# Bias tables read backward from one copy, longer modulation products, and gate rows sent through memory

## The chip, the cores and the metric

The kernel runs on one core of one Trainium2 chip. Times are microseconds (us) of device time of one launch. TensorE (PE in the profile) multiplies matrices and PEld is its weight load; VectorE (DVE), ScalarE (ACT) and GpSimd (POOL) compute and copy; SyncE (SP) and, in this kernel, also ACT and POOL issue DMA transfers, which 16 DMA engines carry out.

## The reference

Two layers of a hybrid block and one layer of a second block act on 256 tokens of width 2048, all in float32.

```
for layer in range(2):                      # first block
    proj = x @ w_in[layer]                  # 2048 -> 7680, split into 11 parts
    ya = diff_attention(q, k, v, bias)      # 4 heads; bias by distance from rel_bias
    yb = dilated_attention(q, k, v, bias)   # 8 heads; bias by distance
    yc = conformer_conv(...)                # 31 taps, layer norm, 512 x 512
    x = layer_norm(ALPHA * x + concat(ya, yb, yc) @ w_out[layer])
# second block
mod = silu(c) @ w_mod + b_mod               # six vectors of 2048: shifts, scales, two gates
h = modulate(rms_norm(x), mod[0], mod[1])
# neighbourhood attention (bias rpb[head, row offset, column offset]), Fourier, pooling
# and short-convolution branches, merged through sigmoid gates into y
x = x + mod[2] * (y @ w_o)
x = x + mod[5] * swiglu(modulate(rms_norm(x), mod[3], mod[4]))
```

Three parts matter here. The attention heads of the first block add a bias that depends on query minus key position alone, so a head's table is a row of 384 numbers, laid out shifted by one for each query partition. The neighbourhood attention adds such a bias by column offset. The two gate vectors `mod[2]` and `mod[5]` multiply every token's row, so they are wanted as 2048 numbers on each of 128 partitions.

## The kernel before, in words

All weights stream once through SBUF. A job is a weight piece of 512 KB (256 rows by 512 columns), loaded by SP into `raw` (four buffers), split by ACT into a high part `hi` (line 343) and by DVE into the rest `lo` (line 351). A step of the program multiplies one job by the transposed activations: twelve matmuls of 512 columns (hi by high, lo by high, hi by low, for two halves of the rows and two token tiles) into the PSUM tile `mm`. ACT and DVE work up to four steps ahead of TensorE (`LOOK`). There are 892 jobs and as many steps, in the order in which `run` writes them out; every engine takes its own instructions in that order.

Everything else is a side task, a generator that is advanced by one link per step: attention heads, transposes, convolution, norms. Some of them let a step pass when a meter of DVE's work (`room`) says that DVE is behind; the meter counts about 1.04 ns for each element and 0.065 us for each DVE call, so fewer calls can move such work to an earlier step.

The modulation product `mod` is computed on DVE. `wmod_step` takes a job of [128, 1024] numbers of `w_mod` (tile `wm`, two buffers, loaded by SP) and multiplies and sums it against the vector `c` (spread over all partitions) into the accumulator `wsum`. There are 192 jobs, in six chunks that `WMOD_STEPS` spreads over the steps; chunks 0 and 1 are done for two vectors, so there are 256 products of 1024. `wmod_end` finishes a chunk; for chunks 2 and 5, the gates, it makes the tiles `gb` (2048 numbers on each partition).

`bias_tables`, added at step 20, makes the first block's tables. It computes the 12 rows `r` of 384 numbers, writes them to memory as `scr` and reads the three tables `T` from it. `tables`, at step 220, does the like for the second block: it writes `rpbs`, from which `na_head` reads a piece `rpb` twice for each pair of a head and a query tile. POOL issues all of these, in order with its small norm computations (`rstd`) and the residual transfers (`res`, `xs`). `causal` and `na_head` add the tables to the scores on DVE.

Of the kernel before, what the change touches and what calls it, by code (L numbers as in the profile page):

```python
# [18 lines left out]
D = 2048  # L19
# [13 lines left out]
# the order in which the normed (group, token tile) pieces are transposed, and how many a group's use waits for  # L33
TILES = [(0, 0), (1, 0), (0, 1), (1, 1), (2, 0), (2, 1), (3, 0), (3, 1)]
READY = [3, 4, 6, 8]
# the part of the program (in steps) over which each chunk of the modulation's product is spread
# [18 lines left out]
class Meter:  # L55
    """Passes calls on to an engine and adds up about how long they hold it, in us."""
# [30 lines left out]
class Task:  # L87
    """A generator that emits a side chain of the program, a link per step."""
# [24 lines left out]
class Block:  # L113
    """One block of output columns: all of its contraction, for its token tiles."""
# [14 lines left out]
class Kernel:  # L129
# [47 lines left out]
    def room(self):  # L177
        """Time left on the vector engine until the tensor engine is through this step."""
        return self.t_pe + 2.6 - self.t_dve
# [4 lines left out]
    def need(self, t, items=1 << 30):  # L184
        """Emits what is left of a task (or its first items). A task between steps holds no more than
        its `rows` of the row buffers and its `banks` of the four, and what has begun stays within them."""
        if t.done or t.items >= items:
            return
        if t in self.tasks:
            self.tasks.remove(t)  # L190
        if t not in self.running:
            while self.held()[0] + t.rows > ROWS or self.held()[1] + t.banks > 4:
                self.need([r for r in self.running if not r.busy][0])
            self.running.append(t)
        was, t.forced = t.forced, True
        while not t.done and t.items < items:
            t.step()
        t.forced = was
        if t.done:
            self.running.remove(t)  # L200

    def wait(self, me, deps):
        """Lets steps pass until the tasks are done."""
        while not all(t.done for t in deps):
            if me().forced:
                for t in deps:
                    self.need(t)
                break
            yield
# [14 lines left out]
    def rstd(self, var, n, scale, eps):  # L224
        """(var * scale + eps) ** -0.5 for [128, n]."""
# [6 lines left out]
    def split_t(self, items, ahead=0):  # L232
        """Transposes [128 tokens, 512] pieces and splits them. items: (src, hi, lo, scale, bias),
        src a function that gives the piece; scale and bias: [128, 4] columns or None."""
# [72 lines left out]
    def order(jobs):  # L307
        """Steps of four (job, half of its contraction, token tile) each, and the step after which each job's
        operands are free. At the tail of a block its first token tile goes ahead of the second."""
# [96 lines left out]
    def wmod_init(self):  # L406
        """silu(c) @ w_mod + b_mod on the vector engine, 128 of its elements at a time."""
# [7 lines left out]
        self.wm_junk = self.cp.tile([128, 512], BF16, name="wmjunk")  # L415
# [22 lines left out]
    def wmod_step(self, force=False):  # L438
# [14 lines left out]
        if f == 0 and k == 0:  # L453
            self.need(self.wm_task)
            self.wm_sum = [self.m([128, 16, 4], name="wsum", bufs=3) for _ in range(2 if chunk < 2 else 1)]
        t = self.wm_raw.pop(i)
        for v, acc in enumerate(self.wm_sum):
            for q in range(2):
                x = slice(q * 512, (q + 1) * 512)
                nc.vector.tensor_tensor_reduce(out=self.wm_junk, in0=t[:, x], in1=self.wm_c[v][k][:, x], scale=1.0,  # L460
                                               scalar=0.0, op0=ALU.mult, op1=ALU.add,
                                               accum_out=acc[:, f, 2 * k + q:2 * k + q + 1])
# [5 lines left out]
    def wmod_end(self, chunk, sums):  # L468
# [17 lines left out]
        if chunk in (2, 5):  # L486
            yield
            for g in range(4):
                if g % 2 == 0:
                    row = self.modc[(chunk, g // 2)] = self.s([128, 1024], name="gb")  # L490
                p = self.aux()
                for j in range(4):
                    nc.tensor.matmul(p[:, j * 128:(j + 1) * 128], d[:, g * 4 + j:g * 4 + j + 1].broadcast_to([128, 128]),
                                     self.ident, start=True, stop=True)
                yield
                nc.scalar.activation(row[:, (g % 2) * 512:(g % 2 + 1) * 512], p, AF.Copy)
                yield
# [36 lines left out]
    def bias_tables(self):  # L534
# [14 lines left out]
        # 128 copies of each row, read one short of their pitch: row p comes out shifted by p  # L549
        scr = self.dp.tile([12, 128, 384], F32, name="scr")  # L550
        nc.gpsimd.dma_start(scr, r.unsqueeze(1).broadcast_to([12, 128, 384]))
        self.T = []
        for g in (1, 2, 0):
            t = self.s([128, 4, 256], name="T")
            nc.gpsimd.dma_start(t, bass.AP(scr.tensor, g * 4 * 128 * 384 + 127, [[383, 128], [128 * 384, 4], [1, 256]]))
# [222 lines left out]
    def rms_t(self, r, ss, sc, sh, dst=None, rs=None):  # L778
        """rms norm, scale and shift of token-major r (4 of [128, 2, 512]) into transposed halves."""
# [38 lines left out]
    def qk_t(self, q, k, c, scale):  # L818
        """Transposed q (times scale) and k of one head: [128, 512], q then k."""
# [14 lines left out]
    def causal(self, qk, rows, T, s, m, i):  # L834
        """Negated scores of both query tiles: [128, 384] (tile 1, then tile 0) and their minima."""
# [5 lines left out]
        nc.vector.tensor_tensor_reduce(out=s[:, 0:256], in0=p[:, 0:256], in1=T, scale=1.0, scalar=3e38,  # L841
                                       op0=ALU.add, op1=ALU.min, accum_out=m[:, i:i + 1])
        nc.vector.tensor_tensor_reduce(out=s[:, 256:384], in0=p[:, 256:384], in1=T[:, 128:256], scale=1.0, scalar=3e38,
# [10 lines left out]
    def pv(self, s, v, c):  # L854
        """Probabilities [128, 384] times v: PSUM [128, 256], tile 1 then tile 0."""
# [133 lines left out]
    def second(self):  # L989
# [70 lines left out]
        def tables():  # L1060
            self.rpb = self.dp.tile([56, 64, 127], F32, name="rpbs")
            nc.gpsimd.dma_start(self.rpb, a["rpb"].unsqueeze(1).broadcast_to([56, 64, 127]))
# [170 lines left out]
    def context(self):  # L1233
        """Normed and modulated context, transposed and split."""
# [14 lines left out]
    def na_head(self, j, hd, x, y, need, me):  # L1249
# [7 lines left out]
        def load(t):  # L1257
            raw = self.h([128, 256], name="rpb")
            for i in range(2):
                off = (hd * 7 + 3 - 2 * t - i) * 64 * 127 + 63  # L1260
                nc.gpsimd.dma_start(raw[i * 64:(i + 1) * 64, :].rearrange("p (a c) -> p a c", a=4),
                                    bass.AP(self.rpb.tensor, off, [[126, 64], [64 * 127, 4], [1, 64]]))
# [16 lines left out]
        for t in range(2):  # L1279
# [9 lines left out]
                                    raw.rearrange("p (a c) -> p a c", a=4), op=ALU.subtract)  # L1289
# [26 lines left out]
    def put_split(self, p, dst, c, scale=None):  # L1316
        """[128, 256] in PSUM into the halves of chunk c."""
# [121 lines left out]
def _constants():  # L1439
# [5 lines left out]
    c["onehot"] = oh  # L1445
# [4 lines left out]
    c["dmask"] = mask  # L1450
# [21 lines left out]
def _layout(i):  # L1472
# [22 lines left out]
    def blocks(w):  # L1495
        """[.., K, N] as [.., N / 512, K / 256, 128, 1024]: what one transfer brings, in one piece."""
# [10 lines left out]
        "ln_g": n["ln_g"], "ln_b": n["ln_b"], "rel_bias": n["rel_bias"], "rpb": rpb.reshape(56, 127),  # L1507
# [25 lines left out]
```

## Time and profile before

| what | value |
|---|---|
| time, median of 3 runs | 2675.42 us (2675.05 to 2678.34) |
| span of the profiled execution, first to last instruction | 2668.7 us |
| median above that span | 6.7 us |
| TensorE busy | 2624.8 us, 98% of the span |
| weight loads busy | 2164.3 us, 81% |
| VectorE busy | 1843.7 us, 69% |
| ScalarE busy | 1260.4 us, 47% |
| mean DMA rate | 231 GB/s |

For the profiled execution no time other than its span is given, so the time around the span (launch and end) is taken as the 6.7 us between it and the median. Busy time of an engine is the union of its instructions' times. Matmuls overlap each other in a pipeline, so two matmuls that start 0.23 us apart each show a duration of 0.39 us, and TensorE can show no idle time while its matmuls start more slowly than they could.

### The profile page before, as it was taken

To read this page: it belongs to the slowest core of one execution; us is meant where nothing else is said; L and a number is where in the kernel's file an instruction comes from. 1 tells how busy PE (TensorE), PEld (TensorE's weight loads), DVE (VectorE), ACT (ScalarE), POOL (GpSimd) and SP (SyncE) were. 2 spreads that over 40 slices of the span, in tenths; PEclk is the share of its full clock that TensorE was granted. 3 is DMA by queue.
4 is the path that set the end of the run, shared out by engine and by line. 5 is a ranking of instruction groups with operands and counts; after the bars stand their busy time and mean duration, and the time that the engine had idled before them with its cause. 6 is when DMAs were issued, how large, how long until landed. Compare 5 with 4: busy or idle time off the path is not lost.

```text
span 2668.7 us, 33167 instructions
## 1 busy us (share of the span) xinstructions
PE 2624.8 (98%) x11962; PEld 2164.3 (81%) x11962; DVE 1843.7 (69%) x3028; ACT 1260.4 (47%) x1609; POOL 126.1 (5%) x188
## 2 busy tenths in 40 slices
PE   9999999989999999999999999999999999999999
PEld 7788888768888888887888888888788888888887
DVE  5699787769988799664756686778554554555444
ACT  6354654435566556454454444444444434443442
POOL 0000010000000111020200000000100000000000
PEclk9999999999999999999999999999999999999999
DMA  8876667577765778785767787788655566556654
GB/s 304 213 231 219 212 225 251 194 221 233 233 227 195 280 268 286 255 256 184 230 224 237 255 283 260 262 289 305 222 181 190 190 237 205 189 190 240 225 194 154
DMA packets 171749, 616.79 MB, mean 231 GB/s; under 512 B 19994, under 2 KB 20788, under 8 KB 171584
## 3 DMA queue, kind: packets, MB, share of 16 engines
q1 hardware_dynamic: 158400, 572.59, 64.0%
q0 software_dynamic: 11744, 39.29, 5.3%
q10 hardware_dynamic: 1440, 2.79, 0.3%
q8 instruction: 94, 1.54, 0.2%
q14 instruction: 71, 0.58, 0.1%
HBM read 599.64 MB, written 16.76 MB: 231 GB/s over the span
## 4 chain that ended last, share of the span: by engine, by line
PE 87%; DVE 5%; DMA 4%; issue 2%; ACT 1%; POOL 0%; SPq 0%; ACTq 0%; DVEq 0%; POOLq 0%
PE mm L75 82%; PE aux L75 6%; DMA raw<-in_w_in 3%; DVE lo L351 2%; DVE f L75 1%; DVE wmjunk L75 1%; DVE cacc L75 1%; DMA raw<-in_w_out 1%; ACT hi L343 0%; DVE res L75 0%; DMA row<-in_ln_b 0%; DMA row<-in_ln_g 0%; DVE hcTl L75 0%; POOL rstd L229 0%; DVE bn L75 0%
## 5 line engine op out<-in xcount | busy, mean ns | idle before, releaser
L351 DVE TENSOR_TENSOR lo<-raw,hi 128x1024 fp32r<-128x1024 f32 (+1 forms) x893 | 1077.0, 1220 | 629.9 <-ACT hi L343 627.2
L343 ACT ACTIVATE hi<-raw 128x1024 fp32r<-128x1024 f32 (+1 forms) x893 | 937.5, 1059 | 1067.4 <-PE mm L75 777.7
L75 PE MATMUL mm<-hi,xTh 128*128 128x512 f32 x960 | 388.0, 404 | 18.3 <-ACT hi L343 18.3
L75 PE MATMUL mm<-lo,xTh 128*128 128x512 f32 x960 | 379.0, 395 | 3.5 <-DVE lo L351 3.5
L75 PE MATMUL mm<-hi,xTl 128*128 128x512 f32 x960 | 379.1, 395 | 0.6 <-DVE xTl L75 0.6
L75 DVE CUSTOM_DVE_ANT_0 wmjunk<-wm,c 128x512 bf16<-128x512 f32 x512 | 352.9, 689 | 13.1 <-DMA wm<-in_w_mod 1.9
L75 PE MATMUL mm<-hi,hTh 128*128 128x512 f32 x864 | 343.9, 398 | 0.0
L75 PE MATMUL mm<-hi,hTl 128*128 128x512 f32 x864 | 337.1, 390 | 0.0
L75 PE MATMUL mm<-lo,hTh 128*128 128x512 f32 x864 | 336.6, 390 | 0.0
L75 PE MATMUL mm<-hi,h2Th 128*128 128x512 f32 x704 | 275.9, 392 | 1.1 <-ACT h2Th L284 1.1
L75 PE MATMUL mm<-hi,h2Tl 128*128 128x512 f32 x704 | 274.4, 390 | 1.1 <-DVE h2Tl L75 1.1
L75 PE MATMUL mm<-lo,h2Th 128*128 128x512 f32 x704 | 274.2, 389 | 0.0
L75 PEld LDWEIGHTS mm<-hi,xTh 128*128 128x128 f32 x960 | 183.0, 191 | 57.9 <-ACT hi L343 20.0
L75 PEld LDWEIGHTS mm<-lo,xTh 128*128 128x128 f32 x960 | 183.2, 191 | 42.0 <-DVE lo L351 6.4
L75 PEld LDWEIGHTS mm<-hi,xTl 128*128 128x128 f32 x960 | 182.6, 190 | 40.5 <-DVE xTl L75 1.3
L75 PEld LDWEIGHTS mm<-hi,hTl 128*128 128x128 f32 x864 | 162.2, 188 | 34.5
L75 PEld LDWEIGHTS mm<-lo,hTh 128*128 128x128 f32 x864 | 162.5, 188 | 32.4 <-issue 0.2
L75 PEld LDWEIGHTS mm<-hi,hTh 128*128 128x128 f32 x864 | 162.4, 188 | 32.3 <-issue 0.2
L75 PEld LDWEIGHTS mm<-hi,h2Tl 128*128 128x128 f32 x704 | 132.2, 188 | 29.0 <-DVE h2Tl L75 1.5
L75 PEld LDWEIGHTS mm<-hi,h2Th 128*128 128x128 f32 x704 | 132.2, 188 | 28.3 <-ACT h2Th L284 1.6
L75 PEld LDWEIGHTS mm<-lo,h2Th 128*128 128x128 f32 x704 | 132.3, 188 | 26.9
L75 PE MATMUL mm<-hi,yTh 128*128 128x512 f32 x384 | 151.2, 394 | 0.0
(273 smaller groups left out, 3094.9 us busy)
## 6 DMA issues: line engine op xcount, KB each, us to landing
raw<-in_w_in SPq DMA_DIRECT2D x360, 512.0 KB, 4.4
wm<-in_w_mod SPq DMA_DIRECT2D x192, 512.0 KB, 4.7
raw<-in_w_gate SPq DMA_DIRECT2D x128, 512.0 KB, 4.5
raw<-in_w_fg SPq DMA_DIRECT2D x88, 512.0 KB, 4.3
raw<-in_w_fu SPq DMA_DIRECT2D x88, 512.0 KB, 3.9
raw<-in_w_fd SPq DMA_DIRECT2D x88, 512.0 KB, 4.2
raw<-in_w_out SPq DMA_DIRECT2D x64, 512.0 KB, 4.6
raw<-in_w_o SPq DMA_DIRECT2D x32, 512.0 KB, 5.1
```

The source lines that it names most:

```text
L75: return f(*args, **kw)
L343: nc.scalar.activation(hi[:, k], t[:, k], AF.Copy)
L351: nc.nc.vector.tensor_tensor(lo[:, k], t[:, k], hi[:, k], op=ALU.subtract)
```

## The change

1. The table rows are computed in reverse order (the constants `onehot` and `dmask` are reversed). They are written to memory once (12 rows of 384 numbers) where there were 128 copies of each, and `T` reads a window that starts one number later for each partition. `causal` then reads `T` backward along its columns.
2. `rpb` comes reversed from the host, and `na_head` reads its pieces straight from that input; the copy `rpbs` is gone. The DVE subtraction reads `raw` backward.
3. A modulation product of 1024 is one DVE operation instead of two of 512.
4. For the gates, one matmul turns the [128, 16] vector into 16 rows of 128, ACT copies them to `grow`, a DMA writes them to memory as `g`, and two broadcast DMAs read `gb` from it. Before, 16 matmuls of 128 columns and four ACT copies for each gate made the same numbers on the chip.

```diff
@@ wmod_step
-            self.wm_sum = [self.m([128, 16, 4], name="wsum", bufs=3) for _ in range(2 if chunk < 2 else 1)]
+            self.wm_sum = [self.m([128, 16, 2], name="wsum", bufs=3) for _ in range(2 if chunk < 2 else 1)]
         t = self.wm_raw.pop(i)
         for v, acc in enumerate(self.wm_sum):
-            for q in range(2):
-                x = slice(q * 512, (q + 1) * 512)
-                nc.vector.tensor_tensor_reduce(out=self.wm_junk, in0=t[:, x], in1=self.wm_c[v][k][:, x], scale=1.0,
-                                               scalar=0.0, op0=ALU.mult, op1=ALU.add,
-                                               accum_out=acc[:, f, 2 * k + q:2 * k + q + 1])
+            nc.vector.tensor_tensor_reduce(out=self.wm_junk, in0=t, in1=self.wm_c[v][k], scale=1.0, scalar=0.0,
+                                           op0=ALU.mult, op1=ALU.add, accum_out=acc[:, f, k:k + 1])
@@ wmod_end, chunks 2 and 5
-            for g in range(4):
-                if g % 2 == 0:
-                    row = self.modc[(chunk, g // 2)] = self.s([128, 1024], name="gb")
-                p = self.aux()
-                for j in range(4):
-                    nc.tensor.matmul(p[:, j * 128:(j + 1) * 128], d[:, g * 4 + j:g * 4 + j + 1].broadcast_to([128, 128]),
-                                     self.ident, start=True, stop=True)
-                yield
-                nc.scalar.activation(row[:, (g % 2) * 512:(g % 2 + 1) * 512], p, AF.Copy)
-                yield
+            p = self.aux()
+            nc.tensor.matmul(p[0:16, 0:128], d, self.ident, start=True, stop=True)
+            yield
+            r = self.m([16, 128], name="grow", bufs=2)
+            nc.scalar.activation(r, p[0:16, 0:128], AF.Copy)
+            yield
+            g = self.dp.tile([1, D], F32, name=f"g{chunk}")
+            nc.gpsimd.dma_start(g.rearrange("o (f e) -> (o f) e", e=128), r)
+            yield
+            for i in range(2):
+                row = self.modc[(chunk, i)] = self.s([128, 1024], name="gb")
+                nc.gpsimd.dma_start(row, g[:, i * 1024:(i + 1) * 1024].broadcast_to([128, 1024]))
+            yield
+            yield
@@ bias_tables
-        scr = self.dp.tile([12, 128, 384], F32, name="scr")
-        nc.gpsimd.dma_start(scr, r.unsqueeze(1).broadcast_to([12, 128, 384]))
+        scr = self.dp.tile([12, 384], F32, name="scr")
+        nc.gpsimd.dma_start(scr, r)
...
-            nc.gpsimd.dma_start(t, bass.AP(scr.tensor, g * 4 * 128 * 384 + 127, [[383, 128], [128 * 384, 4], [1, 256]]))
+            nc.gpsimd.dma_start(t, bass.AP(scr.tensor, g * 4 * 384 + 1, [[1, 128], [384, 4], [1, 256]]))
@@ causal (the 128-column operation alike)
-        nc.vector.tensor_tensor_reduce(out=s[:, 0:256], in0=p[:, 0:256], in1=T, scale=1.0, scalar=3e38,
+        nc.vector.tensor_tensor_reduce(out=s[:, 0:256], in0=p[:, 0:256], in1=T[:, ::-1], scale=1.0, scalar=3e38,
@@ second
-            self.rpb = self.dp.tile([56, 64, 127], F32, name="rpbs")
-            nc.gpsimd.dma_start(self.rpb, a["rpb"].unsqueeze(1).broadcast_to([56, 64, 127]))
@@ na_head
-                                    bass.AP(self.rpb.tensor, off, [[126, 64], [64 * 127, 4], [1, 64]]))
+                                    bass.AP(a["rpb"].tensor, off, [[1, 64], [127, 4], [1, 64]]))
...
-                                    raw.rearrange("p (a c) -> p a c", a=4), op=ALU.subtract)
+                                    raw.rearrange("p (a c) -> p a c", a=4)[:, :, ::-1], op=ALU.subtract)
```

On TensorE the order of all other matmuls is as it was. The first place is the first gate burst, in the stage of the `w_gate` weights; `wcol` is the gate vector, `aux` the PSUM tile of side tasks. Before:

```order
L75 MATMUL mm<-hi,hTl 128x512
L75 MATMUL aux<-ident,wcol 128x128 x4
L75 MATMUL mm<-hi,hTh 128x512
L75 MATMUL mm<-lo,hTh 128x512
L75 MATMUL mm<-hi,hTl 128x512
```

and with the change:

```order
L75 MATMUL mm<-hi,hTl 128x512
L75 MATMUL aux<-ident,wcol 16x128
L75 MATMUL mm<-hi,hTh 128x512
L75 MATMUL mm<-lo,hTh 128x512
L75 MATMUL mm<-hi,hTl 128x512
```

There were four such bursts of four matmuls for each gate; one matmul for each gate is left, and nothing else moved.

The second place is POOL at the first block's tables; `mk` is a constant, `rstd` the first norm after them. Before:

```order
L541 DMA mk<-in_dmask 12x384
L551 DMA scr<-r 1536x1x384
L555 DMA T<-scr 128x4x256 x3
L228 ISA
L228 TENSOR_SCALAR rstd<-cmv 128x1
```

and with the change:

```order
L542 DMA mk<-in_dmask 12x384
L553 DMA scr<-r 12x384
L557 DMA T<-scr 128x4x256 x3
L228 ISA
L228 TENSOR_SCALAR rstd<-cmv 128x1
```

The order is the same, and the first transfer writes 12 rows where it wrote 1536. Where the second block's copy `rpbs` stood, POOL has nothing in its place.

The third place is POOL at the end of the second block's `w_o` stage, with the change. `xs_o` and `res` are the residual's transfers, `rstd` belongs to the norm ahead of the last stage, and all rows but the two of line 492 and 496 stood there before in the same order.

```order
L1177 DMA xs_o<-res 128x512 x2
L1158 DMA res<-xs_8043 128x2x512
L492 DMA g_15278<-grow 16x128
L496 DMA gb<-g_15278 128x1024 x2
L1177 DMA xs_o<-res 128x512 x2
L1158 DMA res<-xs_8043 128x2x512
L228 TENSOR_SCALAR rstd<-tot 128x1
```

Three DMAs of the second gate are thus ahead of the last residual transfers and of that norm. Those of the first gate stand in a long stretch in which POOL has nothing else.

## Rows read from the trace of the kernel before

**Rows 1.** The page: span, and TensorE's busy time and weight loads

```profile
span 2668.7 us, 33167 instructions
...
PE 2624.8 (98%) x11962; PEld 2164.3 (81%) x11962; DVE 1843.7 (69%) x3028; ACT 1260.4 (47%) x1609; POOL 126.1 (5%) x188
```

**Rows 2.** The chain that ended last, in order of time: start us, us, what

```profile
84.80 26.66 DMA raw<-in_w_in
...
565.53 25.66 DMA raw<-in_w_in
...
2606.99 57.17 PE mm L75 x252
```

**Rows 3.** POOL in order of time: start us, us, instruction, idle before and releaser

```profile
75.29 1.11 POOL L551 DMA_DIRECT2D scr<-r  x1 [72.23 <-DVE r L75]
111.92 2.29 POOL L555 DMA_DIRECT2D T<-scr  x3 [35.53 <-DMA scr<-r]
...
560.28 1.72 POOL L1062 DMA_DIRECT2D rpbs<-in_rpb  x1
```

**Rows 4.** DMA issues: name, queue, count, KB each, median us to landing

```profile
c<-in_c ACTq DMA_DIRECT2D x4, 512.0 KB, 11.0
...
scr<-r POOLq DMA_DIRECT2D x1, 2304.0 KB, 36.4
...
rpbs<-in_rpb POOLq DMA_DIRECT2D x1, 1778.0 KB, 30.5
T<-scr POOLq DMA_DIRECT2D x3, 512.0 KB, 5.7
```

**Rows 5.** TensorE in order of time, where the two stalls begin

```profile
98.41 0.39 PE L75 MATMUL mm<-hi,xTl 128*128 128x512 f32 x1
...
578.93 0.39 PE L75 MATMUL mm<-hi,xTl 128*128 128x512 f32 x1
588.57 0.80 PE L75 MATMUL mm<-hi,xTh 128*128 128x512 f32 x1 [9.26 <-ACT hi L343]
```

**Rows 6.** Windows: length; busy (count) of PE PEld DVE ACT POOL; clock, DMA share, GB/s

```profile
98.41:128.50 30.09, 24.59 (x88) 18.10 (x86) 17.79 (x31) 11.34 (x12) 2.29 (x3) 0.89 0.85 248
579.15:604.00 24.85, 15.13 (x58) 11.81 (x58) 13.53 (x24) 9.46 (x10) 0.00 (x0) 0.79 0.66 199
2000.00:2100.00 100.00, 100.00 (x451) 82.83 (x450) 48.37 (x44) 44.05 (x47) 0.00 (x0) 1.00 0.58 189
130.00:400.00 270.00, 269.23 (x1282) 221.71 (x1281) 237.22 (x515) 152.51 (x252) 11.26 (x16) 1.00 0.68 222
```

**Rows 7.** TensorE in order of time at the first gate burst

```profile
1710.38 1.05 PE L75 MATMUL aux<-ident,wcol 128*128 128x128 f32 x8
1711.19 0.48 PE L75 MATMUL mm<-hi,hTh 128*128 128x512 f32 x1
1711.50 0.39 PE L75 MATMUL mm<-lo,hTh 128*128 128x512 f32 x1
```

**Rows 8.** DVE by shape: busy us, mean ns, idle before and releaser

```profile
L351 DVE TENSOR_TENSOR lo<-raw,hi 128x1024 fp32r<-128x1024 f32 x891 | 1075.7, 1221 | 629.3 <-ACT hi L343 626.6
L75 DVE CUSTOM_DVE_ANT_0 wmjunk<-wm,c 128x512 bf16<-128x512 f32 x512 | 352.9, 689 | 13.1 <-DMA wm<-in_w_mod 1.9
L75 DVE DVE_READ_ACCUMULATOR2_ANT wsum<- 128x1 f32 x512 | 42.0, 82 | 0.0
L75 DVE CUSTOM_DVE_ANT_0 sc<-aux,T 128x256 f32<-128x256 f32 x32 | 13.4, 419 | 3.2 <-PE aux L75 3.2
L75 DVE CUSTOM_DVE_ANT_0 sc<-aux,T 128x128 f32<-128x128 f32 x32 | 9.1, 285 | 0.0
L75 DVE TENSOR_TENSOR pad<-namask,rpb 128x256 f32<-128x256 f32 x16 | 6.7, 420 | 0.1
```

**Rows 9.** TensorE's waits: line, released by: us in total, times, longest

```profile
PE mm L75 <- DVE lo L351: 3.5, 6, 0.8
```

**Rows 10.** POOL at the norm ahead of the last stage, in order of time

```profile
1918.70 0.18 POOL L228 TENSOR_SCALAR rstd<-tot 128x1 f32<-128x1 f32 x1 [14.74 <-DVE tot L75]
```

More of the change, by code (lines that the diff above doesn't have):

```diff
@@ L414, in wmod_init @@
             self.modc[v] = self.cp.tile([128, 16], F32, name=v)
-        self.wm_junk = self.cp.tile([128, 512], BF16, name="wmjunk")
+        self.wm_junk = self.cp.tile([128, 1024], BF16, name="wmjunk")
     def wmod_rows(self):
@@ L840, in causal @@
         yield
-        nc.vector.tensor_tensor_reduce(out=s[:, 0:256], in0=p[:, 0:256], in1=T, scale=1.0, scalar=3e38,
+        nc.vector.tensor_tensor_reduce(out=s[:, 0:256], in0=p[:, 0:256], in1=T[:, ::-1], scale=1.0, scalar=3e38,
                                        op0=ALU.add, op1=ALU.min, accum_out=m[:, i:i + 1])
-        nc.vector.tensor_tensor_reduce(out=s[:, 256:384], in0=p[:, 256:384], in1=T[:, 128:256], scale=1.0, scalar=3e38,
+        nc.vector.tensor_tensor_reduce(out=s[:, 256:384], in0=p[:, 256:384], in1=T[:, 0:128][:, ::-1], scale=1.0, scalar=3e38,
                                        op0=ALU.add, op1=ALU.min, accum_out=m[:, i + 1:i + 2])
@@ L1259, in load @@
             for i in range(2):
-                off = (hd * 7 + 3 - 2 * t - i) * 64 * 127 + 63
+                off = (hd * 7 + 3 - 2 * t - i) * 127
                 nc.gpsimd.dma_start(raw[i * 64:(i + 1) * 64, :].rearrange("p (a c) -> p a c", a=4),
-                                    bass.AP(self.rpb.tensor, off, [[126, 64], [64 * 127, 4], [1, 64]]))
+                                    bass.AP(a["rpb"].tensor, off, [[1, 64], [127, 4], [1, 64]]))
             return raw
@@ L1444, in _constants @@
     oh[_bucket(np.maximum(d, 0)), j] = -1.0
-    c["onehot"] = oh
+    c["onehot"] = oh[:, ::-1]
     mask = np.zeros((12, 384), np.float32)
@@ L1449, in _constants @@
     mask[4:] = np.where(cnt > 0, -np.log(np.maximum(cnt, 1.0)), BIG)
-    c["dmask"] = mask
+    c["dmask"] = mask[:, ::-1]
     cc = np.arange(64)
@@ L1506, in _layout @@
         "dlam": n["diff_lambda"].reshape(DEPTH, 256), "gain": n["diff_head_gain"], "cols": cols,
-        "ln_g": n["ln_g"], "ln_b": n["ln_b"], "rel_bias": n["rel_bias"], "rpb": rpb.reshape(56, 127),
+        "ln_g": n["ln_g"], "ln_b": n["ln_b"], "rel_bias": n["rel_bias"], "rpb": rpb[:, :, ::-1].reshape(56, 127),
         "ctx": n["ctx_2"][0], "c": np.stack([n["c_2"][0], n["c_ctx_2"]]), "w_in2": blocks(n["w_in_2"][0]),
```

## The prediction

> **What bounds the kernel now.** I read the page first. TensorE is busy for 2624.8 of 2668.7 us [rows 1], so every other engine matters only where it makes TensorE wait or start its matmuls late. Busy time says little about how late: a matmul shows 0.39 us although the next can start 0.23 us after it. So the measure is the rate of starts. The chain's last long piece has 252 matmuls in 57.17 us [rows 2], 0.2269 us each with nothing in the way, and whatever a stretch takes beyond 0.2269 us for each of its matmuls is lost.
>
> The Trainium skill (Perfetto Trace Analysis, Identifying the Most-Contended Engine) says the same of the page's figure: busy time of matmuls is a bad measure of how close TensorE is to its limit, and busy time of weight loads a good one. By busy time 43.9 us of the span are open. By weight loads, 82.83 us in each 100 us of a clean stretch [rows 6], the 2164.3 us need 2613 us, and 56 us are open. The trace bears the rule out in the two stretches below: their idle time is 15.2 us, their starts are 22 us late.
>
> Then I read the chain that ended last for places where it leaves TensorE. Its two longest pieces elsewhere are both a load of weights: 26.66 us from 84.80 and 25.66 us from 565.53 [rows 2]. POOL's own order shows what ran beside them. The 128 copies `scr` were issued at 75.29, and POOL waited for them until 111.92; the 64 copies `rpbs` were issued at 560.28 [rows 3] and took 30.5 us to land, 36.4 us for `scr` [rows 4]. Both late loads end as the copy ends (111.5 and 591.2). The chain runs from load to `hi` to `lo` to matmul: at 588.57 TensorE had waited 9.26 us for ACT's `hi` [rows 5]. ACT and DVE were waiting too; the DMA engines were the bound.
>
> **The change part by part.** *The `scr` copies.* TensorE ran freely until 98.41 [rows 5]. From there to 128.50, where the last late `lo` is past, 30.09 us hold 88 matmuls [rows 6], one or two of them begun before. At 0.2269 us they need 19.5 to 20.0 us, so 10.1 to 10.6 us are lost; I take 10.4. This includes the matmuls that ran at the lower clock level: the granted clock averaged 0.89 there (1.2 GHz instead of 2.4 for part of it), after TensorE had waited. In their place one write of 12 rows is left, and the three `T` loads of 512 KB that follow it come some 30 us earlier. Those were there before and landed in 5.7 us. Do they now starve the stream? After `scr` was issued it took 23.1 us (75.29 to 98.41) until TensorE noticed: that is the lead of loaded and split weights. The nearest rows for such loads are 5.7 us for `T` and 11.0 us for the four broadcasts `c` of 512 KB [rows 4], both shorter than the lead. I take zero; the other end is the old stall in proportion, 11.0/36.4 of 10.4, or 3 us.
>
> *The `rpbs` copies.* From 579.15, just after the last matmul on time, to 604.00, 24.85 us hold 58 matmuls [rows 5, 6], which need 13.2 us; 11.7 us are lost, granted clock 0.79 (again the lower level, after the wait). The copy goes and nothing takes its place. The 32 `rpb` loads keep their number and size and only change the address, so they cost what they did. The tiny mask transfer behind the copy on POOL only gains.
>
> *The gates.* A burst of four matmuls (eight instructions in the trace) starts at 1710.38, where a weight matmul would have started. The next one starts at 1711.19 and the one after it 0.31 us later instead of 0.23 [rows 7]: 0.81 + 0.08 = 0.89 us for a burst, 7.1 us for eight. TensorE has no slack there, so this is time on the path. Two bursts of a quarter of the size stay: between 0.22 us each (in proportion) and 0.45 (half of it fixed); I take 0.3. The gain is 6.5 us, from 6.2 to 6.7. The eight ACT copies go as well, hidden work. Added are a small write and two broadcasts of 512 KB for each gate. Their cover is the same lead of 23 us against at most 11.0 us (I take zero, the other end is 3 us as above). POOL waits until the write has landed. Behind the second gate's DMAs on POOL are the residual's transfers and then the norm that opens the last stage; before that norm POOL sat idle for 14.74 us [rows 10], and by the rows for larger transfers a write needs under 6 us. If the chain took longer than that idle time, each further us would be lost once.
>
> *The modulation products.* The operation of 512 takes 689 ns and reading its sum 82; DVE's nearest row of 1024 is `lo`, 1221 ns [rows 8]. So 256 products fall from 2 x 771 to 1303 ns, 61 us of DVE in all; if the custom operation had no fixed part (1378 ns), 21 us. TensorE waited for `lo` for 3.5 us in six waits [rows 9], and most of these lie in the two stalls already counted. So this is worth about zero on the path, 1 us at most. DVE's meter counts one call less for each product, which lets the residual's scaling in layer 1 come a step or two earlier; it may then wait some us for its DMA, inside the lead.
>
> *Backward reads.* 64 operations on `T` and 16 on `rpb` read one operand from its end: 13.4 + 9.1 + 6.7 = 29.2 us of DVE at their forward durations [rows 8]. No row shows a backward read. The lower end is no change. The upper end is a doubling: 11.2 us for each layer's heads. Between 130 and 400 us DVE has 270 - 237 = 33 us free [rows 6], and the shorter products free about 10 us more (the first chunk's 64 products save 0.239 us each, 15 us over steps 22 to 146, and some two thirds of these lie there), so doubled reads would still be hidden. I take zero on the path. The Trainium skill (SBUF — State Buffer, Door 1: The DMA port swizzle) says that consecutive accesses within a 16-byte line run at full bandwidth, which would make a step of minus one as cheap as plus one; no run shows it yet.
>
> Sum: 10.4 + 11.7 + 6.5 = 28.6 us. The span becomes 2640.1 us, and with the 6.7 us around it, which the change doesn't touch, the time is 2646.8 us against 2675.4 (ratio 0.989).
>
> **The rivals.** *The stalls come back in part.* The early `T` loads follow the `c` loads more closely, and the stream may not have its full lead when they come; the gate broadcasts fall into stages that load fast already. For it: DMA was at 0.85 in the window of the first stall. Against it: 23 us of lead and loads of 11 us. All three bounds together (`T`, and the broadcasts of two gates) cost 3 + 3 + 3 = 9 us: 2656 us.
>
> *DVE is next.* Without the stalls, TensorE could reach the rate at which DVE delivers `lo` in the heads' stretches, where DVE is busy for 237 of 270 us. If the 22 us were given back there, only the gates' 6.5 us would be left: 2669 us. Against it: DVE has 12% free and gets lighter, and the waits for `lo` outside the stalls are near zero.
>
> *More than the sum.* After each stall DVE and ACT refill their lead while heads want them, and small waits follow. If they go too, with a us from the shorter products, some 5 us: 2642 us.
>
> *Slower: backward reads are served at a fraction of the rate.* DVE then becomes the bound in both layers' heads. To undo the gain, each layer would have to lose 14.3 us beyond the 33 + 10 us that DVE has free, 57 us on 11.2 us of work: from six times the forward duration on, the kernel is slower; at seven times each layer loses 24 us, and the time is about 2695 us. No row speaks for such a factor; against it is that the forward operation takes 134 ns for 128 more columns [rows 8], a plain 1.05 ns for each, so a backward read need only deliver one number in that time.
>
> **How the numbers follow.** The sum as forecast has 0.70, stalls in part 0.14, more than the sum 0.07, DVE next 0.05, backward reads far slower 0.02, and something unforeseen 0.02. The range that leaves out no more than 2 in 10 reaches from the third rival, less 2.5 us for the spread of the runs shown, to the first: 2639.5 to 2656.5 us. A change within 0.2%, 5.4 us, is about what a measurement of this kernel can't tell from none. Nearly all cases end faster than that; half of DVE next and half of the unforeseen count as the same: faster 0.93, same 0.04, slower 0.03.
>
> **What would show it.** In the changed kernel's trace: no load of weights over 20 us in the chain; no drop of the granted clock between 95 and 130 us or near 580; windows there with a matmul each 0.23 us; `T` issued within a few us of `scr`; the products near 1.22 us, 256 of them; `sc<-aux,T` at 419 and 285 ns, `pad` at 420; a gate burst of two instructions; POOL idle before the norm's `rstd` as before. The prediction is wrong if TensorE now waits for `lo` in the heads' stretches, if loads starve the stream near 90 us instead, or if the gate's broadcasts delay weights near 1720 or 1900 us.

## The result, and the profile after

| kernel | median, us | range, us | runs | ratio to the kernel before |
|---|---|---|---|---|
| before | 2675.83 | 2675.05 to 2678.34 | 4 | |
| changed | 2643.69 | 2641.83 to 2645.34 | 4 | 0.9882 (95%: 0.9867 to 0.9896) |

The changed kernel is 32.1 us faster, where 28.6 us were forecast. It was timed twice more in later batches: 2642.37 us at 0.9884 (0.9868 to 0.9900), and 2642.19 us at 0.9883 (0.9868 to 0.9897). Below, a gain in us is a ratio's distance from 1 times 2675; an interval of a ratio is 3 to 5 us to each side, so the difference of two kernels is uncertain by some 5 us. The profiled execution of the first experiment took 6819 us, with a matmul only each 0.60 us from its first stretch on, ahead of what the edit touches, and is left out.

The head of the page of the changed kernel, which answers to [rows 1]:

```profile
span 2640.9 us, 32555 instructions
...
PE 2611.5 (99%) x11902; PEld 2155.8 (82%) x11902; DVE 1802.6 (68%) x2516; ACT 1257.7 (48%) x1603; POOL 132.0 (5%) x193
```

The chain that ended last, in order of time (start us, us, what):

```profile
71.32 49.21 PE mm L75 x216
...
505.54 10.03 issue
516.86 9.26 DMA row<-in_ln_b
538.21 57.17 PE mm L75 x252
...
861.75 9.41 DMA raw<-in_w_out
```

The two pieces of 26.66 and 25.66 us of waiting for weights [rows 2] are gone. In their places the chain stays on TensorE from 71.32 to 120.53 and from 538.21 to 595.38; no load of weights is in it for more than 9.41 us. Windows over those places and three others (length; busy (count) of PE PEld DVE ACT POOL; clock, DMA share, GB/s):

```profile
95.00:130.00 35.00, 35.00 (x162) 29.16 (x161) 30.59 (x50) 16.26 (x22) 0.00 (x0) 1.00 0.69 221
565.00:595.00 30.00, 30.00 (x135) 24.82 (x134) 29.56 (x47) 12.74 (x14) 0.00 (x0) 1.00 0.80 253
472.00:486.00 14.00, 11.85 (x35) 8.58 (x36) 13.92 (x35) 9.26 (x13) 1.36 (x3) 0.51 0.38 124
130.00:400.00 270.00, 269.48 (x1285) 222.44 (x1284) 224.20 (x406) 150.77 (x245) 12.69 (x16) 1.00 0.68 223
78.00:92.00 14.00, 14.00 (x63) 11.62 (x62) 10.46 (x16) 5.79 (x6) 2.32 (x3) 1.00 0.93 324
```

The first two answer to the stalls of [rows 6]: TensorE busy throughout, 162 matmuls in 35 us and 135 in 30 us, one each 0.22 us with the short ones of side tasks among them, granted clock 1.00 where it had been 0.89 and 0.79. The fifth is where the three `T` loads now run: the DMA engines are busy for 0.93 of it and move 324 GB/s, and TensorE misses nothing. The third is a stall at the border of the two layers that both kernels have, with the clock at its lower level (0.51, 1.2 GHz) after TensorE had waited. POOL in order of time (start us, us, what, [idle before, what ended it]):

```profile
75.53 0.51 POOL L553 DMA_DIRECT2D scr<-r  x1 [72.49 <-DVE r L75]
78.81 2.32 POOL L557 DMA_DIRECT2D T<-scr  x3 [2.77 <-DMA scr<-r]
...
1862.74 0.51 POOL L492 DMA_DIRECT2D g<-grow  x1 [7.92 <-ACT grow L489]
1866.28 1.11 POOL L496 DMA_DIRECT2D gb<-g  x2 [3.03 <-DMA g<-grow]
...
1890.94 0.19 POOL L228 TENSOR_SCALAR rstd<-tot 128x1 f32<-128x1 f32 x1 [13.79 <-DVE tot L75]
```

The `T` loads follow `scr` by 3.28 us instead of 36.63 [rows 3]. The second gate's write made POOL wait for 3.03 us, and POOL was still idle for 13.79 us before the last stage's norm, 14.74 before [rows 10]. DVE by shape (busy us, mean ns, idle before and releaser):

```profile
L75 DVE CUSTOM_DVE_ANT_0 wmjunk<-wm,c 128x1024 bf16<-128x1024 f32 x256 | 312.4, 1220 | 4.7 <-DMA wm<-in_w_mod 2.4
L75 DVE DVE_READ_ACCUMULATOR2_ANT wsum<- 128x1 f32 x256 | 21.1, 83 | 0.0
L75 DVE CUSTOM_DVE_ANT_0 sc<-aux,T 128x256 f32<-128x256 f32 x32 | 13.4, 420 | 6.1 <-PE aux L75 6.1
L75 DVE CUSTOM_DVE_ANT_0 sc<-aux,T 128x128 f32<-128x128 f32 x32 | 9.2, 286 | 0.0
L75 DVE TENSOR_TENSOR pad<-namask,rpb 128x256 f32<-128x256 f32 x16 | 6.7, 421 | 0.1
```

Products and sums took 394.9 us [rows 8] and take 333.5. Operands read from their end take what they took from their start: 420, 286 and 421 ns against 419, 285 and 420. TensorE at the first gate, in order of time:

```profile
1688.68 0.39 PE L75 MATMUL mm<-hi,hTl 128*128 128x512 f32 x1
1689.00 0.39 PE L75 MATMUL aux<-ident,wcol 128*16 128x128 f32 x2
1689.32 0.50 PE L75 MATMUL mm<-hi,hTh 128*128 128x512 f32 x1
1689.65 0.39 PE L75 MATMUL mm<-lo,hTh 128*128 128x512 f32 x1
```

A weight matmul was due at 1688.91 (0.227 us after the row at 1688.68); the next one starts at 1689.32, and the one after it 0.33 us later. By the rule of [rows 7] a small burst costs 0.41 + 0.10 = 0.51 us.

### The profile page after: what moved, and what is told of

Same layout as the page of the kernel before. It is cut to its first block, busy times and chain, and to the rows that moved or that the text cites. A ratio compares the mean times of both kernels' runs of the same rounds, so it can differ in the third digit from the quotient of the medians.

```text
span 2640.9 us, 32555 instructions
## 1 busy us (share of the span) xinstructions
PE 2611.5 (99%) x11902; PEld 2155.8 (82%) x11902; DVE 1802.6 (68%) x2516; ACT 1257.7 (48%) x1603; POOL 132.0 (5%) x193
## 4 chain that ended last, share of the span: by engine, by line
PE 94%; DVE 2%; DMA 2%; issue 1%; POOL 0%; ACT 0%; SPq 0%; DVEq 0%; ACTq 0%; POOLq 0%
PE mm L75 88%; PE aux L75 6%; DMA raw<-in_w_in 1%; DVE lo L351 1%; DMA raw<-in_w_out 1%; DMA row<-in_ln_b 1%; DVE f L75 0%; DVE res L75 0%; ACT hi L343 0%; POOL rstd L229 0%; DVE wmjunk L75 0%; POOL rstd L228 0%; DVE xTl L75 0%; DVE gate L75 0%; DVE h2Tl L75 0%
## 5 line engine op out<-in xcount | busy, mean ns | idle before, releaser
L75 DVE CUSTOM_DVE_ANT_0 wmjunk<-wm,c 128x1024 bf16<-128x1024 f32 x256 | 312.4, 1220 | 4.7 <-DMA wm<-in_w_mod 2.4
```

What stands on the lines that cost most here:

```text
L75: return f(*args, **kw)
```

## The experiments

Each kernel is the changed one with the edit shown. Those under the first four headings undo one part, and the fifth undoes what one part did to the order of work. The text under each heading was on record before its run.

### One table copied 128 times again

```diff
-        scr = self.dp.tile([12, 384], F32, name="scr")
-        nc.gpsimd.dma_start(scr, r)
+        scr = self.dp.tile([12, 128, 384], F32, name="scr")
+        nc.gpsimd.dma_start(scr, r.unsqueeze(1).broadcast_to([12, 128, 384]))
...
-            nc.gpsimd.dma_start(t, bass.AP(scr.tensor, g * 4 * 384 + 1, [[1, 128], [384, 4], [1, 256]]))
+            nc.gpsimd.dma_start(t, bass.AP(scr.tensor, g * 4 * 128 * 384 + 127, [[383, 128], [128 * 384, 4], [1, 256]]))
```

with forward reads of `T` and of the two constants.

> The changed kernel with the 128 copies of the first block's rows put back (forward reads of T with them), everything else as changed. Theory: the copies starve the weight stream, and the stall near 98 us returns whole: the prediction's 10.4 us, with its aftermath 12.7 us by the two traces laid over each other, so 10 to 13 us slower than the changed kernel (about 2655 us), with the load piece of over 20 us back in the chain and a lower granted clock near 101 us. Rival: the stall was the sum of the copies and of the two-part products and gate work around them; then less than 6 us come back.

Measured: 2654.36 us (2651.50 to 2655.57, five executions), ratio 0.9922 (0.9907 to 0.9936). The kernel ran once more, for a trace:

> The version with the 128 copies of the first block's rows put back, once more, for a trace of a usual execution. Theory: about 2654 us, 11 to 12 us slower than the changed kernel; the load piece of over 20 us from about 85 us is back in the chain, and the granted clock falls near 101 us. Rival: the time comes back elsewhere.

Measured: 2651.74 us, ratio 0.9921 (0.9906 to 0.9937), 9.6 us above the changed kernel on the same chip (2642.19). From its chain:

```profile
84.34 27.43 DMA raw<-in_w_in
```

the row of its DMA issues (KB, us to landing):

```profile
scr<-r POOLq DMA_DIRECT2D x1, 2304.0 KB, 36.2
```

and windows over the copy, the last one over the stall as [rows 6] has it:

```profile
85.00:99.00 14.00, 13.54 (x60) 10.89 (x58) 2.02 (x3) 1.51 (x2) 0.00 (x0) 1.00 0.85 151
98.00:112.00 14.00, 9.93 (x27) 6.73 (x25) 4.03 (x6) 2.24 (x3) 0.00 (x0) 0.76 0.82 163
98.39:128.85 30.46, 24.28 (x87) 18.00 (x86) 17.45 (x27) 11.35 (x12) 2.29 (x3) 0.89 0.84 245
```

The stall is back with its place and its price: 9.6 to 10.4 us by the times for a term of 10.4, and 10.7 by the trace, since 87 matmuls at 0.2269 us need 19.7 of the 30.46 us. The rival on record, that less than 6 us come back, is refuted by the trace. While the copy runs the DMA engines are busy for 0.82 to 0.85 of the time and move 151 to 163 GB/s; in the changed kernel's fifth window above, 0.93 busy moved 324.

### The other table copied 64 times again

```diff
+            self.rpb = self.dp.tile([56, 64, 127], F32, name="rpbs")
+            nc.gpsimd.dma_start(self.rpb, a["rpb"].unsqueeze(1).broadcast_to([56, 64, 127]))
```

with the old addresses and forward reads.

> The changed kernel with the 64 copies of the second block's bias rows put back, everything else as changed. Theory: the stall comes back at its place (now near 568 us), 11.7 us as predicted and up to 13 by the two traces: 11 to 13 us slower than the changed kernel, about 2656 us. Rival: the residual's row transfers, which stand just ahead on the same queue and moved earlier with the change, were what starved the stream; then the copies cost under 4 us.

Measured: 2658.23 us (2656.91 to 2661.28), ratio 0.9941 (0.9928 to 0.9954). That is 15.5 us above the changed kernel by ratios, where 11.7 to 13 were forecast. TensorE in order of time:

```profile
575.69 0.80 PE L75 MATMUL mm<-hi,xTh 128*128 128x512 f32 x1 [14.19 <-ACT hi L343]
```

and windows over the copy, the end of the wait, and the whole stall:

```profile
549.00:562.00 13.00, 12.51 (x56) 10.02 (x54) 6.63 (x13) 2.10 (x4) 0.00 (x0) 1.00 0.97 160
570.00:580.00 10.00, 3.84 (x9) 2.71 (x10) 3.32 (x5) 3.17 (x3) 0.00 (x0) 0.51 0.45 163
561.35:595.00 33.65, 19.00 (x76) 15.14 (x76) 18.29 (x29) 11.57 (x12) 0.00 (x0) 0.80 0.69 204
```

TensorE waited for 14.19 us here and for 9.26 us in the execution that the forecast was read from [rows 5]; the lower clock follows the wait in both. By the prediction's measure 76 matmuls need 17.2 of the 33.65 us, so 16.4 us are lost in this execution, where 11.7 were lost in that one. The stall is the same; its length differed between the two executions that were profiled with it. The rival on record, that the residual's row transfers starved the stream, is refuted: they are in the changed kernel too, and the wait comes back with the copy alone.

### The old gate bursts again

```diff
-            p = self.aux()
-            nc.tensor.matmul(p[0:16, 0:128], d, self.ident, start=True, stop=True)
...
+            for g in range(4):
+                if g % 2 == 0:
+                    row = self.modc[(chunk, g // 2)] = self.s([128, 1024], name="gb")
+                p = self.aux()
+                for j in range(4):
+                    nc.tensor.matmul(p[:, j * 128:(j + 1) * 128], d[:, g * 4 + j:g * 4 + j + 1].broadcast_to([128, 128]),
+                                     self.ident, start=True, stop=True)
+                yield
+                nc.scalar.activation(row[:, (g % 2) * 512:(g % 2 + 1) * 512], p, AF.Copy)
+                yield
```

> The changed kernel with the gate rows made by 16 matmuls and four ScalarE copies for each gate again. Theory: eight bursts of 0.89 us against two small ones, 6.2 to 6.7 us slower than the changed kernel, about 2650 us, spread in steps of 0.8 to 0.9 us near 1690 and 1860 us. Rival: the broadcast transfers give part of it back by delaying weights, and undoing them costs less than 4 us.

Measured: 2647.97 us (2645.12 to 2649.99), ratio 0.9900 (0.9885 to 0.9915), 4.5 us above the changed kernel by ratios with overlapping intervals. Its burst costs what it did before, 0.81 us to the next matmul and 0.09 behind it:

```profile
1684.91 1.05 PE L75 MATMUL aux<-ident,wcol 128*128 128x128 f32 x8
1685.72 0.48 PE L75 MATMUL mm<-hi,hTh 128*128 128x512 f32 x1
1686.04 0.39 PE L75 MATMUL mm<-lo,hTh 128*128 128x512 f32 x1
```

Eight of 0.89 less two of 0.51 us make 6.1 us. Laid over the changed kernel's trace, matmul by matmul, this one falls behind by 6.3 us at the two gates. The times agree with the direction and do not tell 4.5 from 6.1; the rival on record, that the broadcasts give part of it back, has no support in the traces.

### Products of 512 again

```diff
-            nc.vector.tensor_tensor_reduce(out=self.wm_junk, in0=t, in1=self.wm_c[v][k], scale=1.0, scalar=0.0,
-                                           op0=ALU.mult, op1=ALU.add, accum_out=acc[:, f, k:k + 1])
+            for q in range(2):
+                x = slice(q * 512, (q + 1) * 512)
+                nc.vector.tensor_tensor_reduce(out=self.wm_junk, in0=t[:, x], in1=self.wm_c[v][k][:, x], scale=1.0,
+                                               scalar=0.0, op0=ALU.mult, op1=ALU.add,
+                                               accum_out=acc[:, f, 2 * k + q:2 * k + q + 1])
```

The tiles for the sums and for the discarded products have their old sizes again.

> The changed kernel with each modulation product as two operations of 512 again (and with that the order of before on every engine), copies and gates as changed. Theory: VectorE's 61 us are off the path, so this is as fast as the version with the old meter and products of 1024: 2637 to 2639 us, and 5 us faster than the changed kernel, whose order of VectorE's work is what costs. Rival: the shorter products are worth a few us where heads and splits crowd VectorE; then it is slower than the version with the old meter by 2 us or more.

Measured: 2640.42 us (2638.40 to 2641.47), ratio 0.9875 (0.9861 to 0.9888), beside 2642.37 for the changed kernel on the same chip. Undoing this part makes the kernel no slower; by medians it is 2 us faster, where 5 were forecast. The changed kernel ran again in the same batch:

> The changed kernel once more, unedited, as the yardstick of this group of runs. Both theories: 2643 to 2645 us, and a profile whose stall at the border of the two layers (10 us, lower clock for 10 to 14 us) may differ by some us from the first one.

### Products of 1024 in the old order

The longer products also move work, since DVE's meter counts one call less for each. Here the meter is given the missing call, and every engine has the order of before outside the parts that the change rewrote:

```diff
+            self.t_dve += 0.065
```

behind each product in `wmod_step`.

> The changed kernel with 0.065 us added to VectorE's meter for each product, so that the meter counts as it did and every instruction stands in the order of before, the products being still one operation of 1024. Theory: two small stalls that the changed kernel's trace shows and before's did not (1.5 us near 531 us, 2.8 us near 986 us) come from the residual's scaling and one product moving ahead in VectorE's order; with the old order they shrink and the kernel is 2.5 to 4.5 us faster than the changed one, about 2640 us. Rival: the two are chance (GpSimd's norm operations took longer there, 2.66 against 1.68 us), and the time is that of the changed kernel within 1.5 us.

Measured: 2637.71 us (2634.86 to 2638.70), ratio 0.9861 (0.9847 to 0.9875). Since this came from another batch than the changed kernel's, both ran side by side:

> The version with the old meter and products of 1024 once more, on the same chip as the changed kernel in this group. Theory: VectorE's order costs the changed kernel 1.5 to 2 us near 531 us at least, and by the medians so far 4.7 to 6 us: 2636 to 2639 us against 2642 to 2644 us. Rival: the gap is one chip's luck and shrinks below 2 us.

> The changed kernel, unedited, as the partner of the version with the old meter on the same chip. Both theories: 2641 to 2645 us.

Measured: 2640.36 (2639.07 to 2642.11), ratio 0.9876 (0.9862 to 0.9891), against 2642.19 (2641.86 to 2642.39), ratio 0.9883. It is the fastest version by its medians, 1.8 us in this batch, where 4.7 to 6 were expected and the rival said below 2; its gain over the changed kernel is too small for the intervals. Beside the kernel with products of 512, which has the same order, its ratios are 0.9861 and 0.9876 against 0.9875: a gain in time from the 61 us that DVE is spared does not show beyond the intervals. Where the gain lies shows in TensorE's waits (released by: us in total, times, longest) of the changed kernel

```profile
PE aux L75 <- ACT xr L792: 7.4, 2, 4.4
...
PE aux L75 <- DVE sg L75: 1.8, 2, 1.6
```

and of this one:

```profile
PE aux L75 <- ACT xr L793: 6.8, 2, 4.4
...
PE aux L75 <- DVE sg L75: 0.3, 1, 0.3
```

The wait for `sg` is made on DVE. Its order of time in the changed kernel:

```profile
524.18 0.69 DVE L75 TENSOR_TENSOR res<-res,row 128x512 f32<-128x512 f32 x1 [3.08 <-DMA row<-in_ln_g]
526.21 0.69 DVE L75 TENSOR_TENSOR res<-res,row 128x512 f32<-128x512 f32 x1 [1.34 <-DMA row<-in_ln_b]
...
527.95 1.41 DVE L75 TENSOR_TENSOR res<-res,row 128x512 f32<-128x512 f32 x2
...
530.42 1.28 DVE L75 TENSOR_TENSOR sg<-mm,sg 128x512 f32<-128x512 f32 x2
```

and with the old order:

```profile
522.49 0.69 DVE L75 TENSOR_TENSOR res<-res,row 128x512 f32<-128x512 f32 x1 [3.31 <-DMA row<-in_ln_g]
524.03 0.69 DVE L75 TENSOR_TENSOR res<-res,row 128x512 f32<-128x512 f32 x1 [0.85 <-DMA row<-in_ln_b]
...
525.78 1.28 DVE L75 TENSOR_TENSOR sg<-mm,sg 128x512 f32<-128x512 f32 x2
...
528.11 1.41 DVE L75 TENSOR_TENSOR res<-res,row 128x512 f32<-128x512 f32 x2
```

The second pair of the residual's scaling stands ahead of `sg` in the changed kernel and behind it with the old order, and TensorE transposes `sg`. The waits for the row's DMAs ahead of the first pair are there in either order (3.08 and 1.34 us, 3.31 and 0.85). The longest wait for `sg` was 1.2 to 1.6 us in all three profiles of the changed kernel and at most 0.4 us in the three with the old order (this kernel's two, and that with products of 512). In total the waits for `sg` are 1.5 to 1.8 us against 0.3 to 0.6, so about 1.2 us of the 2 are shown, with one exception: the kernel of the next heading has the changed order too, and its longest wait for `sg` was 0.6 us. TensorE's larger waits for `xr`, the second stall that was expected to shrink, are there in either order (6.4 and 6.8 against 7.3 to 7.5), so the order is not their cause.

### Is it the bytes?

The same amount, 2.25 MB, written to DRAM from 128 partitions in pieces of 4 and 2 KB, right behind `scr`:

```diff
+        dump = self.dp.tile([128, 4608], F32, name="dump")
+        for i in range(4):
+            nc.gpsimd.dma_start(dump[:, i * 1024:(i + 1) * 1024], self.wm_c[i // 2][i % 2])
+        nc.gpsimd.dma_start(dump[:, 4096:4608], self.wm_c[0][0][:, 0:512])
```

> The changed kernel with the bytes of the first copy written by nobody's need: 2304 KB from 128 partitions to memory in pieces of 4 KB and 2 KB, issued by GpSimd right behind the one copy of the rows. Theory that bytes are what starves the stream: some 10 us slower than the changed kernel, with a late weight load near 85 us. Rival, that the copies' form does it (short rows, 12 source partitions, 36 us for what should need a quarter of that): the transfers land in about 10 to 15 us together, within the 23 us lead, and the time is that of the changed kernel within 2 us.

Measured: 2641.86 us (2640.37 to 2643.04), ratio 0.9880 (0.9867 to 0.9894): no cost. A window over it:

```profile
77.00:91.00 14.00, 14.00 (x63) 11.60 (x62) 8.53 (x14) 5.19 (x6) 4.46 (x8) 1.00 0.97 347
```

and the window of the kernel before over its copy of the same size:

```profile
85.00:99.00 14.00, 13.79 (x61) 11.08 (x59) 2.02 (x3) 1.28 (x2) 0.00 (x0) 1.00 0.83 150
```

347 GB/s stand against 150. The same bytes in another form leave the weights' stream alone, although the `T` loads queued behind them landed in 16.2 us instead of 8.3. So it was not the amount that starved the stream. Which trait slowed `scr` is not shown: the two copies differ at once in the length of the rows (1.5 KB against 4 and 2 KB), in the partitions read (12 against 128) and in reading each row again.

### Is it the row's length?

The rows of `rpbs` are 508 bytes long. A needless copy of the same shape with rows of 512 bytes, in its place:

```diff
+            dump = self.dp.tile([56, 64, 128], F32, name="dump")
+            nc.gpsimd.dma_start(dump, a["ctx"][0:56, 0:128].unsqueeze(1).broadcast_to([56, 64, 128]))
```

> The changed kernel with a needless copy of 64 times 56 rows of 512 bytes (1792 KB) where the second copy of 64 times 56 rows of 508 bytes stood. Theory that the row of 508 bytes, just under 512, is the trouble: it lands in under 12 us and costs under 2 us. Rival, that any copy into thousands of short rows loads the transfer engines alike: it lands in about 30 us again and costs 11 to 15 us.

Measured: 2665.74 us (2664.98 to 2669.57), ratio 0.9973 (0.9962 to 0.9984), 23 to 24 us above the changed kernel. The copy's row:

```profile
dump<-in_ctx POOLq DMA_DIRECT2D x1, 1792.0 KB, 40.0
```

TensorE behind it:

```profile
581.80 0.79 PE L75 MATMUL mm<-hi,xTh 128*128 128x512 f32 x1 [22.63 <-ACT hi L343]
```

and the window:

```profile
541.00:578.00 37.00, 18.18 (x81) 14.71 (x79) 12.10 (x20) 4.22 (x5) 0.96 (x2) 0.81 0.72 148
```

It starves the stream more than the 508-byte rows did, and more than either expectation had it. The Trainium skill (DMA: Bandwidth & Descriptors, Specifications) gives 512 bytes as the smallest transfer at line rate and says that shorter ones are read, modified and written. This run does not bear that out as the cause: rows of 512 bytes landed in 40.0 us and those of 508 in 30.5 and 33.6, so that limit does not explain the slow copies here.

### Is it reading the same rows again?

The copy of the kernel above with as many rows of 512 bytes, written to the same place, each read from an address of its own:

```diff
-            nc.gpsimd.dma_start(dump, a["ctx"][0:56, 0:128].unsqueeze(1).broadcast_to([56, 64, 128]))
+            nc.gpsimd.dma_start(dump, bass.AP(a["ctx"].tensor, 0, [[128, 56], [56 * 128, 64], [1, 128]]))
```

> The changed kernel with the same needless copy of 3584 rows of 512 bytes into the same place at the same step as in the run with rows of 512 bytes, but every row is read from another place, where that one read each of 56 rows 64 times. Theory that short rows written to memory are slow in themselves: it lands in about 40 us again and costs some 20 us. Rival, that the repeated reading of the same few rows is slow: it lands in under 15 us and costs under 2 us.

Measured: 2643.33 us (2637.35 to 2643.90), ratio 0.9880 (0.9862 to 0.9898): no cost. Its row and its window:

```profile
dump<-in_ctx POOLq DMA_DIRECT2D x1, 1792.0 KB, 15.1
```

```profile
541.00:560.00 19.00, 19.00 (x85) 15.75 (x84) 16.76 (x26) 5.82 (x7) 3.00 (x3) 1.00 0.97 356
```

With the same number and length of rows, 148 GB/s became 356, and TensorE lost nothing. The rows read here fill one stretch without gaps, and those of the copy above begin 8 KB apart; but the rows that `rpbs` copies have no gaps either and landed in 30.5 and 33.6 us, so what is left between slow and fast is that the same rows are read again.

## Why the prediction was right, and where it was off

**The stalls.** Shown: each comes back with its copy alone and goes with it. `scr` was sized right (10.4 against 9.6 to 10.4 by times and 10.7 by the trace). The `rpbs` term of 11.7 holds for the execution that it was read from, in which TensorE waited for 9.26 us, and was too small for others: put back, the wait was 14.19 us and the loss 16.4 by the trace, 15.5 by ratios. (The 58 matmuls of that term count one begun before the window, as the 76 and 87 above do; without it each loss is 0.2 us more.) One profile gives the place of a stall and one sample of its length.

**The early loads.** The step "I take zero" for the `T` loads held: full rate and clock from 78 to 92 us, although the `c` loads needed 11.5 us. The lead of 23 us had room for 2.25 MB more. The first rival, stalls in part, is refuted.

**The gates.** The step that took 0.3 us for the small burst, with an upper bound of 0.45, was low: 0.51. The term is 6.1 to 6.3 by the traces instead of 6.5, and 4.5 by ratios. Broadcasts and POOL's wait cost nothing that shows: idle time of 13.79 us was left ahead of the norm.

**The products.** DVE saved 394.9 - 333.5 = 61.4 us, as forecast (61). The step "about zero on the path" is right for that saving. What its last sentence says of the moved scaling is where it was off: it may wait for its DMA, "inside the lead". The waits for these DMAs are there in either order; the price is that `sg`, which TensorE wants, stands behind a further pair of the scaling. The part costs some 2 us by medians, about 1.2 of them shown.

**Backward reads and DVE as the bound.** Backward reads cost at most 1 ns more each, so the slower rival is refuted. The Trainium skill's rule weighed there (SBUF — State Buffer, Door 1: The DMA port swizzle) agrees with these rows, though they don't show its cause. DVE is busy for 224.2 of 270 us in the heads' stretch, and TensorE's waits for `lo` [rows 9] have no successor: DVE is not the next bound.

**The sum, and what luck there was in it.** The spans differ by 27.8 us, near the 28.6 of the sum. Laid over each other, the n-th matmul of one beside the n-th of the other without the gates' own, the two traces show what this is made of. The changed kernel gains 10.7 us at the first stall, 1.9 near 143 us, 13.0 at the second stall and just behind it, and 6.3 at the gates. It loses 1.2 us at `sg`, 2.5 near 986 us, where TensorE waits for `xr` (2.98 us there against 0.47 before), and some 0.4 in smaller pieces. The sum left out gains of some 3 us and losses of some 4, so a part of its nearness is luck. Why the wait for `xr` grew stays open. The gain near 143 us is a wait that the kernel before had after its first stall,

```profile
154.10 0.72 PE L75 MATMUL aux<-ident,sc 128*128 128x128 f32 x3 [0.44 <-ACT sc L849]
```

and that the changed kernel does not have:

```profile
142.75 1.15 PE L75 MATMUL aux<-ident,sc 128*128 128x128 f32 x9
```

With the `scr` copies alone put back, 0.7 us of the 1.9 return, and with the products of 512 alone nothing: its full size needs both.

**The third rival.** It forecast 2642 us, nearest to the median, from small waits behind the stalls. They are there, 1.9 us near 143 and 0.6 behind the second stall, about half of the 5 us that it gave them. That the median lies so near to it is luck all the same, as the next step shows.

**The time around the span.** This step was wrong, and an error of its own: the 6.7 us were the median less the span of one execution, but the changed kernel's profiled execution took 2642.78 us with a span of 2640.9, 1.9 us apart, and in the other runs 1.7 to 2.2 (1.7 to 1.9 in 28 later executions of the kernel before). So the profiled execution of before was about 5 us quicker than its median. The spans differ by 27.8 us, the medians by 32.1. A longer `rpbs` stall in most executions of the kernel before would account for it; only two profiles have that stall, so this is argued and not shown.

Put back one at a time, the parts are worth 10.4, 15.5, 4.5 and -2.4 us by ratios, 28 of some 31. The 3 us left are within the intervals; what the wait near 143 us has only with two parts at once would be 1.2 of them, and the rest stays open.

## What to carry to other kernels

A copy to DRAM that repeats a few short rows many times can starve a stream of loads far beyond its bytes, as three of them did here; where a table can be read at overlapping addresses, backwards if need be, it isn't needed. Read a stall's place from one profile, its size from several executions, and never take the median less one profile's span for a constant. When operations are merged in a program whose order comes from a meter, give the meter the old count first, and look at what the order does by itself.

## What the hardware showed that was not expected

The DMA engines can be busy and slow at once. During the three repeating copies they were busy for 0.72 to 0.97 and moved 148 to 163 GB/s, while 56 x 64 distinct rows of the same length, or large pieces, ran beside the same stream at 347 to 356. The traces record what the DMA engines carry in packets, here of several rows each. A packet of the repeating copies, of 4 to 4.5 KB, took 0.66 us (`scr`), 0.54 (`rpbs`) and 0.55 (rows of 512 bytes) on average; one of the distinct rows took 0.17 us, and the weights' own packets of 4 KB beside all of these had a median of 0.16 us. That fits with engines held by the copy's packets while the weights waited for their turn, which is argued from these times and not tested. Repetition alone is not slow: the gate's two broadcasts and the `c` loads also read a few rows many times, in rows of 4 KB into on-chip memory, and landed in 5.6 and 11.5 us for 512 KB each. For the copies from DRAM to DRAM the repeated address is what the runs leave; why it is slow there and not in those broadcasts (the length of the rows or the target), what the pitch of 8 KB adds in `ctx`, and which trait made `scr` slow, whose rows come from on-chip memory, was not separated.
